# Block sums of the FFN in rooms shared with the mixers' tiles, first sums formed beside the output projections, input forms ordered behind the token factors

## The chip, the cores and the metric

One Trainium2 chip, one core of it. The metric is the device time of one execution in microseconds (us). The kernel before took 1460.63 us in the median of three runs (1458.15 to 1460.65). All times below that carry a position ("at 398.23") are microseconds from the start of the profiled execution's span.

## The reference, cut to what matters

Two layers on 528 tokens (16 learned meta tokens and 512 of the sequence) of width 1024, in float32. Layer 0 mixes tokens with forgetting attention (FoX, 16 heads of 64), layer 1 with a gated linear recurrence (HGRN2, 8 heads of 128). Behind each mixer stands a gated MLP with a causal convolution of width 3 (hidden width 2816):

```python
for layer in range(DEPTH):
    if layer % 2 == 0:
        h = h + fox_attention(h, ...)      # ends in o @ w_out
    else:
        h = h + hgrn2_mixer(h, ...)        # ends in o @ w_out
    h = h + conv_ffn(h, ...)
return h[:, N_META:]

def conv_ffn(h, ...):
    xn = rms_norm(h, norm_g)
    a = conv_b + causal_dwconv3(xn @ w_gate)
    return (silu(a) * (xn @ w_up)) @ w_down
```

## The kernel before

Activations stand transposed in SBUF: `h` is 128 partitions x 8 blocks x 528 tokens. Every projection is done in split precision: a weight block is loaded into a tile `raw` (SyncE's DMA queue), ScalarE (ACT) casts it to `hi`, VectorE (DVE) forms `lo = raw - hi` (`sub`, L127), and TensorE (PE) multiplies hi by the high part of the input, hi by the low part and lo by the high part (`proj_unit`, L209, L212, L213). There are two rooms for `raw` and three each for `hi` and `lo`, of 128x1024, which the FFN cuts in halves of 128x512.

The program is traced in the order fox, ffn 0, hgrn, ffn 1; the framework's scheduler then lays every instruction into its engine's queue, by program order, dependences and its own simulated timeline. An engine works through its queue strictly in that order, and so do the DMA queues that SyncE (SP) and GpSimd (POOL) issue. `self.after(ins, prev)` adds an order between two instructions that the scheduler must keep.

A mixer ends in an output projection over 8 row blocks m, each with 128x1024 weights `wo` or `ho` (fox: the last loop over m, which calls `out_proj` at L662; the first halves of four blocks are done earlier, at L615; hgrn: the loop behind the last `stage_o`). Each block's result is added to `h`, and `sumsq(m)` builds the squares for the next norm.

The FFN begins with `token_stats` (L301 matmuls give the mean squares; twelve small DVE instructions and a copy into `rst`, L311, give each token's factor 1/rms) and `spread_rs` (L322 matmuls spread the factors over partitions, L324 copies them into `rsb`). The columns of the hidden layer are then worked in pairs. The first pair is done by `plain`: for m = 0, 1 the gate products over 8 blocks in a PSUM bank "s" (`pss`, of which there are four; "p", `psp`, has two; "c" and "d" one each), then DVE multiplies each half by `rsb` into `A` (L1208), the convolution follows, then the up products (L1217). All later pairs go through `seven`: a 2x2 block product in seven products instead of eight (Strassen's scheme, as in Winograd's form), L1143 to L1145. It needs two things more:

- input forms: sums and differences of blocks of `h`, `input_forms(k)` for k = 0 to 3: two ACT scalings, one DVE subtraction (L1071), two DVE instructions (L1075), a cast to `xfhi` and a subtraction into `xflo`;
- weight sums: sums of blocks of the weights, formed by DMA alone in `make_sums`: SP loads one block into a tile `sum` (L1110, 256 KB), then POOL issues a DMA that adds a second block onto it (L1111), the second block from memory or from another sum. Twelve such tiles have a pool of their own, opened with the FFN. Each `next(making)` brings one or two sums; `plain` calls it five times, and `seven` three times for each of its jobs.

At the start of the FFN the rest of SP's queue is therefore made of blocks for `plain` (`raw<-gu`, L1096), a down block (`raw<-dn`) and the first sums.

Of the kernel before, what the change touches and what calls it, by code (L numbers as in the profile page):

```python
# [12 lines left out]
F32 = mybir.dt.float32  # L13
F32R = mybir.dt.float32r
# [3 lines left out]
ALU = mybir.AluOpType  # L18
# [3 lines left out]
P = 128  # L22
D = 1024
KT = D // P
T = 528
# [3 lines left out]
NEARLY = 4  # L29
NSUMS = 12  # L30
PAIRS = [1, 2, 2, 2, 2, 2]
HALF = KT * P // 2
FF = 2816
NF = FF // P
# [49 lines left out]
class Builder:  # L84
# [44 lines left out]
    def setup(self):  # L129
        nc = self.nc  # L130
        cp = self.cp = self.pool("const")
        self.h = cp.tile([P, KT, T], F32, name="h")
        self.vec = cp.tile([P, V_END], F32, name="vec")
        nc.sync.dma_start(self.vec, self.a["vec"])
        self.wraw = self.pool("wraw", 2)
        self.whi = self.pool("whi", 3)
        self.wlo = self.pool("wlo", 3)
        q, k = (self.weights(self.a["wqk"][0, i], KT, parts=2) for i in range(2))
        order = [(q, 0), 0, (k, 0), 1, 2, 3, (q, 1), (k, 1), 4, 5, 6, 7]
        for x in order:  # L140
            if isinstance(x, int):
                nc.sync.dma_start(self.h[:, x, :], self.a["h0"][:, x, :])
            else:
                x[0][3][x[1]]()
        self.first = q[:3], k[:3]
        cst = cp.tile([P, C_END], F32, name="cst")
        self.cst = cst
        nc.sync.dma_start(cst, self.a["cst"])
        self.ident = cst[:, C_ID : C_ID + P]
        self.identr = cp.tile([P, P], F32R, name="identr")  # L150
        nc.vector.tensor_copy(self.identr, self.ident)
        self.xhi = cp.tile([P, KT, T], F32R, name="xhi")
        self.xlo = cp.tile([P, KT, T], F32R, name="xlo")
        self.x = [(self.xhi[:, k, :], self.xlo[:, k, :]) for k in range(KT)]
        self.rsb = cp.tile([P, T], F32, name="rsb")
        self.onesd = cp.tile([P, 2], F32, name="onesd")
        nc.vector.memset(self.onesd, 1.0 / D)
        self.tiny = self.pool("tiny", 2)
        self.sqp = self.pool("sqp", 2)
        self.ps = self.pool("ps", 1, PSUM)  # L160
        self.nbank = 0
        self.ss = None

    def anybank(self):
# [14 lines left out]
    def weights(self, src, n, w=P, parts=1):  # L179
# [19 lines left out]
        return *u, [partial(load, slice(i * m, i * m + m)) for i in range(parts)]  # L199

    def proj_unit(self, ps, units, x, t0, tn, prev=None):

        mm = self.nc.tensor.matmul
        total = sum(u[2] for u in units)
        k = 0
        for hi, lo, n in units:
            for i in range(n):
                xh, xl = (y[:, t0 : t0 + tn] for y in x[k])
                ins = mm(ps, hi[:, i, :], xh, start=k == 0, stop=False)  # L209
                if k == 0 and prev is not None:  # L210
                    self.after(ins, prev)
                mm(ps, hi[:, i, :], xl, start=False, stop=False)  # L212
                mm(ps, lo[:, i, :], xh, start=False, stop=k == total - 1)  # L213
                k += 1
                if k % 2 == 0:
                    yield 0.66

    def lone(self, pool, gcol, t0):

        x = pool.tile([P, KT, 32], F32, name="lone")  # L220
        g = self.vec[:, gcol : gcol + KT].rearrange("p (k o) -> p k o", o=1)
# [74 lines left out]
    def token_stats(self, segs, last=False, bank=None):  # L296
# [13 lines left out]
        y = self.rsqrt(am, "n")  # L310
        nc.vector.tensor_copy(rs, y)  # L311
        return am, rs
# [14 lines left out]
    def fox(self, ctx):  # L327
# [8 lines left out]
        for kt in range(KT):  # L336
            self.sumsq(kt, 0, nc.gpsimd, s2)
        lone = self.lone(sp, V_FOXN, T - 32)
        identb = sp.tile([P, P], BF16, name="identb")
# [236 lines left out]
        for i in range(NSLOT):  # L576
            pk = sp.tile([P, 4, T], F32R, name=f"pk_{i}", tag=f"pk_{i}")
            d = {n: pk[:, j, :] for j, n in enumerate(("k1", "q1", "k2", "q2"))}
# [37 lines left out]

        late = [sp.tile([P, T], F32, name=f"late_{i}") for i in range(4)]
        ox, gated = [], []
# [3 lines left out]
        for p in range(-3, NPAIR):  # L622
# [26 lines left out]
            while gated and p >= max(gated[0], 5 + gated[0] // 4):  # L649
# [5 lines left out]
                self.sub(olo, o, ohi.bitcast(F32))  # L655
                ox.append((ohi, olo))
        for m in range(KT):
            res = None
            if m >= NEARLY:
# [115 lines left out]
    def hgrn(self, ctx):  # L775
# [6 lines left out]
        ohi = sp.tile([P, KT, T], F32R, name="ohi")  # L782
        ogs, ox = [None] * KT, [None] * KT
        lmask = sp.tile([P, len(LEVELS) - 3, 64], I32, name="lmask")
        nc.sync.dma_start(lmask, a["lmask"])
# [39 lines left out]
        self.normsplit(V_HGN)  # L825
        lone = self.lone(sp, V_HGN, 0)
        am, rs = self.token_stats(SEGH)
# [4 lines left out]
        def stage_a(m):  # L832

            if m % 2 == 0:
                vv = s2.tile([P, 5, 2 * P], F32, name="vv", tag="vv", bufs=3)
                vals[m] = vals[m + 1] = vv
# [7 lines left out]
            f = s2.tile([P, T], F32, name="f", tag="f", bufs=3)  # L844
            kp = s2.tile([P, T], F32, name="kp", tag="kp", bufs=3)
            qp = s2.tile([P, T], F32, name="qp", tag="qp", bufs=4)
# [168 lines left out]
        for m in range(-3, KT):  # L1015
# [7 lines left out]
                (stage_g(g) if g else None, 5.4 * len(g)),  # L1023
            )
        for m in range(KT):
            wt = self.weights(a["ho"][m], KT)
            for t0, tn in late:
# [8 lines left out]
    def ffn(self, ctx, layer, a0, o0):  # L1036
# [10 lines left out]
        s2 = self.pool(f"ffn2_{layer}", 2, ctx=ctx)  # L1047
        sums = self.pool(f"sums_{layer}", 1, ctx=ctx)

# [14 lines left out]
        def input_forms(k):  # L1064
# [3 lines left out]
            for x, kt in ((u[:, 0:8:7, :], k), (u[:, 1:3, :], 4 + k)):  # L1068
                h = self.h[:, kt, g0:].rearrange("p (f t) -> p f t", t=gw)
                nc.scalar.activation(x, h, AF.Copy, scale=self.vcol(gcol + kt))  # L1070
            nc.vector.tensor_tensor(  # L1071
                u[:, 3:6:2, :], u[:, 0:3:2, :], u[:, 7:8, :].to_broadcast([P, 2, gw]), ALU.subtract
            )
            for i, x, y in ((4, 3, 2), (6, 4, 1)):
                nc.vector.scalar_tensor_tensor(u[:, i, :], u[:, x, :], -1.0, u[:, y, :], ALU.mult, ALU.subtract)  # L1075
# [22 lines left out]

        def hidden_blocks(job):

            j, i = job
            return [a[f"gu{layer}"][2 * j + m, i, k] for m in range(2) for k in range(2)]

        def make_sums():

            def new(job, f, x, y):
                s = sums.tile([P, HALF], F32, name="sum", tag="sum", bufs=NSUMS)
                nc.sync.dma_start(s, x)  # L1110
                nc.gpsimd.dma_start(s, y, accum_op=ALU.add)  # L1111
                made[job, f] = s

            for n_, job in enumerate([*jobs, None]):
                if job is not None:
                    w11, w12, w21, w22 = hidden_blocks(job)
                    new(job, 1, w21, w22)
                    new(job, 3, w11, w21)
                    yield
                if n_:  # L1120
                    new(jobs[n_ - 1], 4, hidden_blocks(jobs[n_ - 1])[1], made[jobs[n_ - 1], 2])
                    yield
                if job is not None:
                    new(job, 2, w11, made[job, 1])
                    yield

        jobs, made = [], {}
        making = make_sums()

        def seven(j, i, put):  # L1130
# [5 lines left out]
            job = j, i  # L1136
            w11, w12, _, w22 = hidden_blocks(job)

# [8 lines left out]

            u, v = block(w11), parts(made[job, 1])
            yield product(A, u, 0, True)
            nc.scalar.copy(B, A)  # L1150
            yield product(D, v, 3, True)
            put(1, 1, D, False)
            u, v = parts(made[job, 2]), block(w12)
            next(making, None)
            yield product(B, u, 4, False)
# [3 lines left out]
            put(0, 0, A, True)  # L1159
            u, v = parts(made[job, 3]), parts(made[job, 4])  # L1160
            next(making, None)
            yield product(C, u, 5, False)
# [3 lines left out]
            u = block(w22)  # L1166
            next(making, None)
            yield product(C, u, 6, False)
# [30 lines left out]
        def plain(j, out):  # L1199

            A, t = new_pair("A"), new_pair("t")[:, :, :n]
            for m in range(2):
                wg = [block(a[f"gu{layer}"][2 * j + m, 0, k]) for k in range(2)]
                next(making)
                for t0, tn in ga:
                    ps = self.bank("s")[:, :tn]
                    yield from self.proj_unit(ps, wg, self.x, t0, tn)
# [3 lines left out]
                wu = [block(a[f"gu{layer}"][2 * j + m, 1, k]) for k in range(2)]  # L1211
                next(making)
                for t0, tn in up:
# [4 lines left out]
                input_forms(2 * m + 1)  # L1218
            next(making)
            split(t, out)  # L1220
# [60 lines left out]
        for r in PAIRS:  # L1281
            runs.append((j0, r, []))
            j0 += r
        for j in range(PAIRS[0], NF // 2):
            jobs += [(j, 0)] if j == PAIRS[0] else []
            jobs += [(j + 1, 0)] if j + 1 < NF // 2 else []
            jobs += [(j, 1)]
        side = None
# [115 lines left out]
```

## Time and profile before

| | |
|---|---|
| three runs, us | 1458.15, 1460.63, 1460.65 |
| the profiled execution, us | 1461.63 |
| its span, us | 1459.8 |
| its mean granted PE clock | 0.992 |
| start of ffn 0 (L301 matmuls) | at 391.63 |
| start of ffn 1 (L301 matmuls) | at 1114.30 |

The span is the time between the first and the last instruction of the profiled execution; 1.8 us lie around it. In the windows of the profile, an engine's busy time in a stretch is followed by the number of instructions that touch it, then come the granted PE clock, the busy share of the 16 DMA engines (it can pass 1 where transfers of two queues overlap on an engine) and the rate. In the chain of waits and the timeline, each row is a start, a duration and what ran; "SPq" and "POOL ... DMA_DIRECT2D" are issues of transfers, "x7" says that neighbours of one kind are put together.

### The profile page before, as it was taken

What the parts mean: (1) busy time and instruction counts of PE and PEld (TensorE: products, weight loads), DVE (VectorE), ACT (ScalarE), POOL (GpSimd) and SP (SyncE); (2) the same over time, 40 slices, a digit from 0 to 9 for tenths busy, and PEclk for the clock granted to TensorE, in tenths of its full rate; (3) what the DMA queues carried; (4) which work ended last, traced back from release to release, by engine and by line L of the source; (5) the groups of instructions that cost most, each with busy time, mean ns of one, the idle gap of its engine ahead of it and who ended that gap; (6) DMA issues with size and microseconds to landing.
All of it is one profiled execution on the core that took longest, in us unless ns stands there. A gap on an engine that the chain in (4) does not pass through costs nothing.

```text
span 1459.8 us, 29803 instructions
## 1 busy us (share of the span) xinstructions
PE 1419.5 (97%) x11368; PEld 1338.7 (92%) x11368; DVE 1010.4 (69%) x2263; ACT 723.9 (50%) x1524; POOL 175.3 (12%) x280
## 2 busy tenths in 40 slices
PE   7999999999979999999999999999999999999999
PEld 6888888888979999999999999999999999999997
DVE  7555545775858877767775667677648887777774
ACT  5455555574636555554643224333436665555551
POOL 7000000000122221221000000000020221221100
PEclk9999999999989999999999999999999999999999
DMA  4433344412689998886322202121284899988823
GB/s 160 120 106 90 95 108 125 128 60 62 194 195 238 231 232 194 218 208 164 92 69 87 77 13 88 59 73 45 64 226 129 200 260 225 218 218 219 200 80 101
DMA packets 104887, 206.90 MB, mean 142 GB/s; under 512 B 14104, under 2 KB 16920, under 8 KB 104744
## 3 DMA queue, kind: packets, MB, share of 16 engines
q1 hardware_dynamic: 81704, 163.05, 36.7%
q0 software_dynamic: 23040, 41.95, 17.2%
q8 instruction: 89, 1.46, 0.4%
q14 instruction: 54, 0.44, 0.1%
HBM read 168.53 MB, written 2.10 MB: 117 GB/s over the span
## 4 chain that ended last, share of the span: by engine, by line
PE 90%; DMA 4%; DVE 2%; ACT 2%; SPq 1%; issue 1%; ACTq 0%; DVEq 0%
PE pss L209 7%; PE pss L212 7%; PE pss L213 7%; PE psp L209 7%; PE psp L213 7%; PE psp L212 7%; PE psp L258 6%; PE psp L1143 5%; PE psp L1144 5%; PE psp L1145 5%; PE psd L1143 3%; PE psd L1144 3%; PE psd L1145 3%; PE psc L752 2%; PE pss L906 1%; PE psc L1143 1%
## 5 line engine op out<-in xcount | busy, mean ns | idle before, releaser
L127 DVE TENSOR_TENSOR lo<-raw,hi 128x512 fp32r<-128x512 f32 (+2 forms) x318 | 254.4, 804 | 95.7 <-ACT hi L1089 50.3
L1089 ACT CAST hi<-raw 128x512 fp32r<-128x512 f32 (+1 forms) x232 | 139.1, 604 | 169.6 <-PE pss L212 53.8
L209 PE MATMUL psp<-xhi,hi 128*128 128x264 f32 (+2 forms) x752 | 216.8, 290 | 6.1 <-ACT xhi L278 6.1
L212 PE MATMUL psp<-xlo,hi 128*128 128x264 f32 (+2 forms) x752 | 216.9, 289 | 3.3 <-DVE xlo L279 3.3
L213 PE MATMUL psp<-xhi,lo 128*128 128x264 f32 (+2 forms) x752 | 217.2, 289 | 0.0
L212 PE MATMUL pss<-room,hi 128*128 128x264 f32 (+2 forms) x532 | 169.7, 320 | 0.0
L209 PE MATMUL pss<-room,hi 128*128 128x264 f32 (+2 forms) x532 | 168.8, 320 | 0.0
L213 PE MATMUL pss<-room,lo 128*128 128x264 f32 (+2 forms) x532 | 168.7, 319 | 0.0
L1089 ACT CAST hi<-sum 128x512 fp32r<-128x512 f32 x160 | 99.0, 619 | 111.8 <-PE psd L1144 42.0
L195 ACT CAST hi<-raw 128x1024 fp32r<-128x1024 f32 (+1 forms) x82 | 82.4, 1007 | 141.4 <-PE psp L212 59.8
L209 PEld LDWEIGHTS psp<-xhi,hi 128*128 128x128 f32 x752 | 142.6, 190 | 9.4 <-ACT xhi L278 6.1
L212 PEld LDWEIGHTS psp<-xlo,hi 128*128 128x128 f32 x752 | 142.8, 190 | 5.3 <-DVE xlo L279 3.8
L213 PEld LDWEIGHTS psp<-xhi,lo 128*128 128x128 f32 x752 | 142.8, 190 | 1.5 <-issue 1.5
L1143 PE MATMUL psp<-xhi,hi 128*128 128x264 f32 (+1 forms) x480 | 136.6, 285 | 1.7 <-ACT hi L1089 1.7
L1145 PE MATMUL psp<-xhi,lo 128*128 128x264 f32 (+1 forms) x480 | 136.3, 284 | 1.0 <-DVE lo L127 1.0
L1144 PE MATMUL psp<-xlo,hi 128*128 128x264 f32 (+1 forms) x480 | 136.2, 284 | 0.0
L127 DVE TENSOR_TENSOR lo<-sum,hi 128x512 fp32r<-128x512 f32 x160 | 109.5, 687 | 24.1 <-ACT hi L1089 20.8
L1111 POOL DMA_DIRECT2D sum<-gu x80 | 70.1, 886 | 352.7 <-PE psp L212 96.6
L213 PEld LDWEIGHTS pss<-room,lo 128*128 128x128 f32 x532 | 99.6, 188 | 6.5
L212 PEld LDWEIGHTS pss<-room,hi 128*128 128x128 f32 x532 | 100.0, 188 | 5.1
L209 PEld LDWEIGHTS pss<-room,hi 128*128 128x128 f32 x532 | 99.9, 188 | 4.2
L1270 DVE TENSOR_TENSOR h<-h,pss 128x264 f32<-128x264 f32 (+2 forms) x145 | 73.4, 508 | 35.8 <-PE pss L213 35.3
(442 smaller groups left out, 3961.2 us busy)
## 6 DMA issues: line engine op xcount, KB each, us to landing
sum<-gu SPq DMA_DIRECT2D x160, 256.0 KB
raw<-gu SPq DMA_DIRECT2D x136, 256.0 KB
sum<-gu POOLq DMA_DIRECT2D x80, 256.0 KB, 5.5
sum<-sum POOLq DMA_DIRECT2D x80, 256.0 KB, 5.2
raw<-dn SPq DMA_DIRECT2D x80, 256.0 KB
pk<-stg SPq DMA_DIRECT2D x48, 264.0 KB
raw<-wqk SPq DMA_DIRECT2D x14, 512.0 KB
raw<-wv SPq DMA_DIRECT2D x8, 512.0 KB
```

Of the source, the lines that this page charges most:

```text
L127: self.nc.vector.tensor_tensor(out, x, y, ALU.subtract)
L195: nc.scalar.copy(hi, raw)
L209: ins = mm(ps, hi[:, i, :], xh, start=k == 0, stop=False)
L212: mm(ps, hi[:, i, :], xl, start=False, stop=False)
L213: mm(ps, lo[:, i, :], xh, start=False, stop=k == total - 1)
L258: mm(ps[:tn, :256], y[:, t0 : t0 + tn], w, start=n == 0, stop=n == 23)
L1089: nc.scalar.copy(hi, raw)
L1111: nc.gpsimd.dma_start(s, y, accum_op=ALU.add)
L1143: mm(ps, hi[:, k, :], xh, start=start and k == 0, stop=False, skip_group_check=not start)
L1144: mm(ps, hi[:, k, :], xl, start=False, stop=False, skip_group_check=not start)
L1145: mm(ps, lo[:, k, :], xh, start=False, stop=k == 3, skip_group_check=not start)
L1270: nc.vector.tensor_tensor(hv, hv, ps, ALU.add)
```

## The change

A pool `shared` is opened once for the whole kernel: two tiles "two" of 128x2112 and one tile "one" of 128x1840 floats. The fox mixer uses them for two of its six head slots (`pk_2`, `pk_3`, which heads 14 and 15 use last), three of its four `late` tiles and `lone`; the hgrn mixer for its value tiles `vv`, its keys `kp` and `lone`. The FFN's own pool of twelve sums is gone: `make_sums` cuts the same three tiles into 4 + 4 + 3 = 11 rooms of 128x512.

`make_sums` is now started before the output projection of the mixer, and the loop over m calls `next` from m = 2 on (six calls); `plain` calls it no more. In `plain`, the gate products of m = 1 go to bank "p" instead of "s". The first DVE instruction of `input_forms` is ordered behind the copy into `rst`.

```diff
+        self.shared = self.pool("shared", 1)
...
+    def share(self, dtype=F32):
+        n = 4 * T
+        two = [self.shared.tile([P, n], dtype, name="two", tag="two", bufs=2) for _ in range(2)]
+        return *two, self.shared.tile([P, 3 * T + 256], F32, name="one", tag="one")
...
+    def make_sums(self, layer):
...
+        rooms = cycle(s[:, x : x + HALF] for s in self.share() for x in range(0, s.shape[1] - HALF + 1, HALF))
+        made = self.made = {}
+        def new(job, f, x, y):
+            s = made[job, f] = next(rooms)
+            nc.sync.dma_start(s, x)
+            nc.gpsimd.dma_start(s, y, accum_op=ALU.add)
...
         y = self.rsqrt(am, "n")
-        nc.vector.tensor_copy(rs, y)
+        self.stats = nc.vector.tensor_copy(rs, y)
...
-            pk = sp.tile([P, 4, T], F32R, name=f"pk_{i}", tag=f"pk_{i}")
+            if i in (2, 3):
+                pk = shared[i - 2].rearrange("p (a t) -> p a t", t=T)
+            else:
+                pk = sp.tile([P, 4, T], F32R, name=f"pk_{i}", tag=f"pk_{i}")
...
+        self.making = self.make_sums(0)
         for m in range(KT):
+            if m > 1:
+                next(self.making)
             res = None
...
+        self.making = self.make_sums(1)
         for m in range(KT):
+            if m > 1:
+                next(self.making)
             wt = self.weights(a["ho"][m], KT)
...
-            nc.vector.tensor_tensor(
+            ins = nc.vector.tensor_tensor(
                 u[:, 3:6:2, :], u[:, 0:3:2, :], u[:, 7:8, :].to_broadcast([P, 2, gw]), ALU.subtract
             )
+            self.after(ins, self.stats)
...
-                next(making)
                 for t0, tn in ga:
-                    ps = self.bank("s")[:, :tn]
+                    ps = self.bank("sp"[m])[:, :tn]
...
-                next(making)
                 for t0, tn in up:
...
-            next(making)
             split(t, out)
```

`make_sums` itself is otherwise as it was; in `seven` only `making` became `self.making`.

**SP at the end of fox.** The queue before, from the last head's rows (`lrow`) on: `wo` are the output projection's weights, `res` the residual input, `gu` and `dn` blocks of the FFN.

```order
L194 DMA raw<-wo 128x512
L720 DMA pk_258<-lrow 1x4x128 x2
L721 DMA pk_258<-lrow 2x16
L194 DMA raw<-wo 128x512 x2
L194 DMA raw<-wo 128x1024 x4
L1096 DMA raw<-gu 128x512 x2
L661 DMA res<-h 128x528
L1096 DMA raw<-gu 128x512 x2
L661 DMA res<-h 128x528
L1096 DMA raw<-gu 128x512 x4
L1110 DMA sum<-gu 128x512 x7
L1096 DMA raw<-gu 128x512
```

And of the change, where `two` and `one` are the shared tiles (L226 is the load of a sum, L1152 that of a block):

```order
L200 DMA raw<-wo 128x512
L226 DMA one<-gu 128x512 x2
L769 DMA two<-lrow 1x4x128 x2
L770 DMA two<-lrow 2x16
L226 DMA one<-gu 128x512
L200 DMA raw<-wo 128x512 x2
L226 DMA two<-gu 128x512 x8
L200 DMA raw<-wo 128x1024 x4
L1152 DMA raw<-gu 128x512
L710 DMA res<-h 128x528
L1152 DMA raw<-gu 128x512 x3
L710 DMA res<-h 128x528
```

Two loads of sums moved ahead of the last head's rows, and eight stand in a block ahead of the four large `wo` loads; the seven and five that stood among the FFN's blocks are gone from there.

**SP at the end of hgrn.** Before (`hg` and `ho` are the gate's and the output projection's weights):

```order
L194 DMA raw<-hg 128x1024 x8
L194 DMA raw<-ho 128x1024 x5
L1110 DMA sum<-gu 128x512 x11
L194 DMA raw<-ho 128x1024
L1110 DMA sum<-gu 128x512
L194 DMA raw<-ho 128x1024 x2
L1096 DMA raw<-gu 128x512 x9
```

And of the change:

```order
L200 DMA raw<-hg 128x1024 x7
L226 DMA one<-gu 128x512 x3
L200 DMA raw<-hg 128x1024
L200 DMA raw<-ho 128x1024 x2
L226 DMA two<-gu 128x512 x4
L200 DMA raw<-ho 128x1024
L226 DMA two<-gu 128x512 x4
L200 DMA raw<-ho 128x1024 x5
L1152 DMA raw<-gu 128x512 x9
```

The block of eleven sums ahead of the sixth `ho` load is spread over the loads before it.

**DVE at the start of ffn 0.** Before, from the second Newton step of the token factors on (`run`, `rqn` are its steps, `am` holds the mean squares):

```order
L127 TENSOR_TENSOR lo<-raw,hi 128x512
L291 TENSOR_TENSOR run<-rqn 128x6
L127 TENSOR_TENSOR lo<-sum,hi 128x512
L127 TENSOR_TENSOR xflo<-room,xfhi 128x4x264
L292 SCALAR_TENSOR_TENSOR run<-run,am 128x6
...
L305 MEMSET am 128x1
L311 COPY rst<-rqn 128x6
L324 COPY rsb<-psc 128x256
L127 TENSOR_TENSOR lo<-raw,hi 128x512
L324 COPY rsb<-psd 128x272
L1208 TENSOR_TENSOR A<-pss,rsb 128x264 x2
```

And of the change (L1126 and L1131 are the input forms, L353 and L366 the copies into `rst` and `rsb`, L1232 the multiplication into `A`):

```order
L347 MEMSET am 128x1
L353 COPY rst<-rqn 128x6
L1126 TENSOR_TENSOR room<-room 128x2x264 x4
L1131 SCALAR_TENSOR_TENSOR room<-room 128x264 x2
L126 TENSOR_TENSOR lo<-raw,hi 128x512
L1131 SCALAR_TENSOR_TENSOR room<-room 128x264 x2
L366 COPY rsb<-psc 128x256
L1131 SCALAR_TENSOR_TENSOR room<-room 128x264 x2
L366 COPY rsb<-psd 128x272
L126 TENSOR_TENSOR lo<-two,hi 128x512
L1131 SCALAR_TENSOR_TENSOR room<-room 128x264 x2
L1232 TENSOR_TENSOR A<-pss,rsb 128x264 x2
```

The input forms, which stood ahead of and between the steps of the token factors, follow the copy into `rst` in one block, most of it ahead of the copies into `rsb`.

More of the change, by code (lines that the diff above doesn't have):

```diff
@@ L29 @@
 NEARLY = 4
-NSUMS = 12
 PAIRS = [1, 2, 2, 2, 2, 2]
@@ L199, in weights, with hidden_blocks @@
         return *u, [partial(load, slice(i * m, i * m + m)) for i in range(parts)]
+    def hidden_blocks(self, layer, job):
+        j, i = job
+        return [self.a[f"gu{layer}"][2 * j + m, i, k] for m in range(2) for k in range(2)]
+    def make_sums(self, layer):
+        nc = self.nc
+        jobs = []
+        for j in range(PAIRS[0], NF // 2):
+            jobs += [(j, 0)] if j == PAIRS[0] else []
+            jobs += [(j + 1, 0)] if j + 1 < NF // 2 else []
+            jobs += [(j, 1)]
+        rooms = cycle(s[:, x : x + HALF] for s in self.share() for x in range(0, s.shape[1] - HALF + 1, HALF))
[4 more added lines that the diff above has]
+            nc.gpsimd.dma_start(s, y, accum_op=ALU.add)
+        for n, job in enumerate([*jobs, None]):
+            if job is not None:
+                w11, w12, w21, w22 = self.hidden_blocks(layer, job)
+                new(job, 1, w21, w22)
+                new(job, 3, w11, w21)
+                yield
+            if n:
+                ahead = jobs[n - 1]
+                new(ahead, 4, self.hidden_blocks(layer, ahead)[1], made[ahead, 2])
+                yield
+            if job is not None:
+                new(job, 2, w11, made[job, 1])
+                yield
     def proj_unit(self, ps, units, x, t0, tn, prev=None):
@@ L216, in proj_unit, with lone @@
                     yield 0.66
-    def lone(self, pool, gcol, t0):
-        x = pool.tile([P, KT, 32], F32, name="lone")
+    def lone(self, x, gcol, t0):
+        x = x.rearrange("p (k t) -> p k t", k=KT)
         g = self.vec[:, gcol : gcol + KT].rearrange("p (k o) -> p k o", o=1)
@@ L337, in fox @@
             self.sumsq(kt, 0, nc.gpsimd, s2)
-        lone = self.lone(sp, V_FOXN, T - 32)
+        shared = self.share(F32R)
+        lone = self.lone(shared[2][:, 3 * T :], V_FOXN, T - 32)
         identb = sp.tile([P, P], BF16, name="identb")
@@ L615, in stage_p @@
                 yield from out_proj(m, 0, 4, hold=True)
-        late = [sp.tile([P, T], F32, name=f"late_{i}") for i in range(4)]
+        late = [shared[2][:, i * T : i * T + T] for i in range(3)] + [sp.tile([P, T], F32, name="late")]
         ox, gated = [], []
@@ L783, in hgrn @@
         ogs, ox = [None] * KT, [None] * KT
+        w = 5 * 2 * P
+        shared = self.share()
+        vvs = cycle(x[:, :w].rearrange("p (t c) -> p t c", c=2 * P) for x in shared)
+        kps = cycle(x[:, w : w + T] for x in shared)
         lmask = sp.tile([P, len(LEVELS) - 3, 64], I32, name="lmask")
@@ L825, in hgrn @@
         self.normsplit(V_HGN)
-        lone = self.lone(sp, V_HGN, 0)
+        lone = self.lone(shared[0][:, w + T : w + T + 256], V_HGN, 0)
         am, rs = self.token_stats(SEGH)
@@ L834, in stage_a @@
             if m % 2 == 0:
-                vv = s2.tile([P, 5, 2 * P], F32, name="vv", tag="vv", bufs=3)
+                vv = next(vvs)
                 vals[m] = vals[m + 1] = vv
@@ L844, in stage_a @@
             f = s2.tile([P, T], F32, name="f", tag="f", bufs=3)
-            kp = s2.tile([P, T], F32, name="kp", tag="kp", bufs=3)
+            kp = next(kps)
             qp = s2.tile([P, T], F32, name="qp", tag="qp", bufs=4)
@@ L1047, in ffn @@
         s2 = self.pool(f"ffn2_{layer}", 2, ctx=ctx)
-        sums = self.pool(f"sums_{layer}", 1, ctx=ctx)
         rooms = {}
@@ L1097, in block @@
             return parts(raw)
[L1099 to L1128, printed above, removed]
         def seven(j, i, put):
@@ L1136, in seven @@
             job = j, i
-            w11, w12, _, w22 = hidden_blocks(job)
+            w11, w12, _, w22 = self.hidden_blocks(layer, job)
             def product(ps, unit, f, start):
@@ L1146, in product @@
                 return 1.45
-            u, v = block(w11), parts(made[job, 1])
+            u, v = block(w11), parts(self.made[job, 1])
             yield product(A, u, 0, True)
@@ L1152, in seven @@
             put(1, 1, D, False)
-            u, v = parts(made[job, 2]), block(w12)
-            next(making, None)
+            u, v = parts(self.made[job, 2]), block(w12)
+            next(self.making, None)
             yield product(B, u, 4, False)
@@ L1159, in seven @@
             put(0, 0, A, True)
-            u, v = parts(made[job, 3]), parts(made[job, 4])
-            next(making, None)
+            u, v = parts(self.made[job, 3]), parts(self.made[job, 4])
+            next(self.making, None)
             yield product(C, u, 5, False)
@@ L1166, in seven @@
             u = block(w22)
-            next(making, None)
+            next(self.making, None)
             yield product(C, u, 6, False)
@@ L1283, in ffn @@
             j0 += r
[L1284 to L1287, printed above, removed]
         side = None
```

## The prediction

> **What bounds the kernel now.** I read the page first: PE is busy 97% of the span and makes up 90% of the chain that ended last. The change leaves all arithmetic of PE as it was, so only time in which PE stands still or runs at a lower clock can be won.
>
> ```profile
> PE 1419.5 (97%) x11368; PEld 1338.7 (92%) x11368; DVE 1010.4 (69%) x2263; ACT 723.9 (50%) x1524; POOL 175.3 (12%) x280
> DMA  4433344412689998886322202121284899988823
> PE 90%; DMA 4%; DVE 2%; ACT 2%; SPq 1%; issue 1%; ACTq 0%; DVEq 0%
> sum<-gu POOLq DMA_DIRECT2D x80, 256.0 KB, 5.5
> ```
>
> The waits of PE, grouped by line, say where it stood still (total, times, longest):
>
> ```profile
> PE psd L1278 <- DVE rsb L324: 8.4, 1, 8.4
> PE pss L737 <- DMA pk<-lrow: 3.4, 1, 3.4
> PE psc L322 <- DVE rst L311: 2.3, 2, 2.1
> PE psc L1143 <- ACT psc L1150: 2.2, 1, 2.2
> PE psp L209 <- ACT hi L195: 0.9, 1, 0.9
> ```
>
> The first lies at the start of ffn 0, the second at the end of fox, 2.1 of the third at the start of ffn 1, the last at the end of hgrn. Windows over these places give the size (us; then busy time and instructions of PE, PEld, DVE, ACT, POOL; granted clock; DMA share; GB/s):
>
> ```profile
> 385.00:450.00 65.00, 52.73 (x409) 51.47 (x409) 44.28 (x89) 33.12 (x59) 16.97 (x23) 0.92 0.85 208
> 405.00:410.00 5.00, 1.16 (x10) 0.91 (x8) 0.42 (x1) 0.00 (x0) 0.89 (x2) 0.86 1.11 269
> 410.00:415.00 5.00, 0.44 (x1) 0.29 (x1) 1.50 (x4) 1.19 (x3) 2.65 (x3) 0.50 1.11 256
> 415.00:420.00 5.00, 5.00 (x27) 4.97 (x27) 2.49 (x5) 2.09 (x3) 0.87 (x1) 0.61 1.08 243
> 1080.00:1090.00 10.00, 8.34 (x67) 7.93 (x67) 2.83 (x4) 2.68 (x4) 2.65 (x3) 1.00 1.09 288
> 1120.00:1130.00 10.00, 7.95 (x53) 7.70 (x52) 7.16 (x22) 4.15 (x8) 1.73 (x2) 0.83 0.67 144
> 358.02 0.29 PE L212 MATMUL pss<-pk,hi 128*128 128x264 f32 x1
> 359.98 0.28 PE L212 MATMUL psp<-pk,hi 128*128 128x264 f32 x1
> ```
>
> The last two rows stand 16 matmuls apart: 1.96 / 16 = 0.1225 us a matmul at full clock. Ffn 0: 65 us hold 65 / 0.1225 = 531 matmuls, but the window has 409, so 122 x 0.1225 = **14.9 us are lost**. The other way: 65 - 52.73 = 12.3 idle, and 5 us at 0.61 and 0.44 at 0.50 cost 2.2 more, 14.5 together. Ffn 1: 10 - 8.34 = 1.7 idle at the `ho` weights, 10 - 7.95 = 2.05 at the token factors, and a clock of 0.83 over 10 us costs 1.7: **5.4 us**.
>
> Why ffn 0 stands still is shown by the chain there, and by the queues of SP and POOL (put together in the timeline):
>
> ```profile
> 398.23 14.50 DMA raw<-gu
> 412.81 0.63 ACT hi L1089
> 414.15 0.36 DVE rsb L324
> 387.17 3.44 SPq L1110 DMA_DIRECT2D sum<-gu  x7
> 391.61 3.26 SPq L1110 DMA_DIRECT2D sum<-gu  x5
> 396.04 5.87 SPq L1096 DMA_DIRECT2D raw<-gu  x3
> 392.84 0.17 DVE am L306
> 404.31 0.17 DVE L311 COPY rst<-rqn 128x6 f32<-128x6 f32 x1
> ```
>
> Twelve loads of sums went in front of the blocks `raw` at 396.04 and 398.23; with POOL's additions beside them the DMA share was 1.1 and a block took 14.5 us. DVE, in order, stood at that block's `lo` with the second `rsb` copy behind it, and PE waited for `rsb`. Besides, `rst` took from 392.84 to 404.31, because input forms stood between its steps.
>
> **The change, part by part.** All sums are against the profiled execution's own 1461.63 us (1.0 above the median of the runs; span 1459.8 and 1.8 around it).
>
> *Sums away from the start of ffn 0.* SP issues twelve loads and POOL their additions some 35 us sooner, beside the output projection. The late block is then loaded into a free queue, and the stall at `rsb` with its slow clock goes. What is late next is DVE: it was busy 44.28 us of the window, and 65 - 14.9 = 50.1 us would remain, 88% of it. Its new order puts most of the input forms as a block ahead of the `rsb` copies:
>
> ```profile
> L1071 DVE TENSOR_TENSOR room<-room 128x528 f32<-128x528 f32 x4 | 2.8, 703 | 0.4 <-ACT room L1070 0.4
> L1075 DVE SCALAR_TENSOR_TENSOR room<-room 128x264 f32<-128x264 f32 x8 | 3.3, 426 | 0.0
> L127 DVE TENSOR_TENSOR lo<-raw,hi 128x512 fp32r<-128x512 f32 x11 | 7.5, 686 | 10.2 <-ACT hi L1089 10.1
> ```
>
> 4 x 0.70 + 4 x 0.43 + 0.69 = 5.2 us. Without forms between its steps, `rst` needs its thirteen small instructions at 0.17 and two `lo` at 0.69, 3.6 us: 392.8 + 3.6 = 396.4, ahead of PE, which reaches L322's place after 53 matmuls at 391.6 + 6.5 = 398.1. The first `rsb` copy then ends at about 402 and the evacuations L1208 begin near 404; PE has 48 matmuls of m = 1 in the other bank until 398.1 + 5.9 = 404.0. That cover just holds; each us by which `rst` slips beyond it is a us of PE. With 2.2 (L1143 behind an ACT copy) perhaps left, I leave **2.5 us lost (0.5 to 8)**: -12.4.
>
> *The last head's rows.*
>
> ```profile
> 333.94 1.59 DMA pk<-lrow
> 332.84 0.41 SPq L720
> ```
>
> Two sum loads now issue just ahead of these rows: 0.41 of queue, and half a MB in front of rows that took 1.59. From +0.3 to +1.5; I take **+0.6**, nearer the issue row. PE waits there already, so nothing hides it.
>
> *The large `wo` loads behind eight sums.*
>
> ```profile
> 352.15 8.73 SPq L194 DMA_DIRECT2D raw<-wo  x2
> 358.59 1.59 ACT L195 CAST hi<-raw 128x512 fp32r<-128x512 f32 x2 [4.07 <-PE pss L212]
> q1 hardware_dynamic: 442, 0.82, 70.8%
> q0 software_dynamic: 1073, 1.94, 65.5%
> q1 hardware_dynamic: 1346, 2.36, 44.0%
> ```
>
> The first two: the load of m = 4 issued at 352.15, and its cast was the second of the two that ended at 360.2, so the data were no limit before. The `q` rows are SP's queue from 387 to 391 with little beside it (0.82 MB in 70.8% of 4 us: 0.29 MB/us), then both queues from 396 to 412 (SP 2.36 / 16 = 0.148 MB/us, additions 1.94 / 16 = 0.121). Now eight sums of 0.26 MB go first; they wait for the last reads of the heads' slots, near 349. 2.6 MB until m = 4 is in: at 0.29 alone, with 1.5 us until the first data, 349 + 1.5 + 9 = 359.5, no wait. At 0.148 throughout: 368, and PE, which needs it at 360.7 behind a cast of 1.05, would wait 8.4, and more with the clock: +10. In between: POOL's addition lands 5.5 us after its issue, of which 256 KB at 0.29 are 0.9, so additions start to share near 356; by then 1.6 MB are in, the other 1.0 takes 6.8: 362.8, PE at 363.9. That is 3.2 late; less 0.5 of slack, plus a chance of the half clock that followed such a wait: **+3.6 (0 to +10)**. The rest of the fox end has cover: a block of m is 48 matmuls, 5.9 us, and its 0.52 MB at 0.148 are 3.5.
>
> A page's rule on the price: the Trainium skill, "DMA: Bandwidth & Descriptors", section "Latency and other measured facts", gives a first byte about 1 us after a GpSimd issue. By it the additions would share from 353 on, m = 4 would land at 365.5, and this term would be about +6.5; the landing row's 5.5 us speaks against it.
>
> *Sums at the end of hgrn.* There they issue ahead of `ho` loads with tens of us to spare, and the stall of 1.7 goes; `rst` no longer stands behind input forms, and the 2.05 with their 1.7 of clock go. Both places keep DVE's block of forms; I leave 1 us (0 to 3): **-4.4**.
>
> On the clock: the row 1120 to 1130 shows a clock of 0.83 around a wait of 2.1 us. The Trainium skill, "TensorE: Matmul & The Clock Gate", "What's actually happening", has the lower clock after at least one idle window of about 3.4 us. By the page alone the 2.1 us would have cost no clock, and this term would be -2.7; the trace's row disagrees, and I go by the row.
>
> The shared rooms cost nothing elsewhere: each tile's readers end well before its next writer, except at the two places above. Eleven rooms in place of twelve matter in `seven` alone, where SP's order is unchanged.
>
> Sum: -12.4 + 0.6 + 3.6 - 4.4 = -12.6; 1461.63 - 12.6 = **1449.0 us**.
>
> **The rivals.**
>
> *The fox end costs nothing.* The sums are in before the additions share (359.5 above), and both starts close: 1461.63 - 14.4 + 0.3 - 5.4 = 1442, down to 1440. For it: the DMA digits of the page are 2 to 6 in the slices of the fox end. Against: 2.1 MB in one block.
>
> *The fox end gives half back.* 368 for m = 4: 1461.63 - 12.4 + 0.6 + 10 - 4.4 = 1455.4, up to 1457.5. For it: at 1.1 share SP's queue kept 0.148 for 16 us. Against: additions chain on one another and start late.
>
> *Slower: the jam moves, and ffn 0 keeps its stall.* From 349 to 388 SP has 2.9 MB of sums, 2.1 of `wo`, 0.5 of `res` and 2.4 of blocks to bring, 7.9 in all. Additions of 2.9 MB at 0.121 last 24 us, SP gets 3.6 MB in them, and the remaining 4.3 at 0.29 take 15: 39 us, to 388, just when ffn 0 needs its blocks. If the rates are lower than these, the blocks land past 400, the `lo` between the forms holds the `rsb` copies as before, and the loss of 14.9 stays on top of +10: 1461.63 + 0.6 + 10 - 4.4 = 1468. It decides from a landing of about 400 on. Against it: from 352 to 386 the page's DMA digits leave half of the engines free.
>
> *The change doesn't do what it says.* The stall of 14.9 was not the sums' doing but the FFN's own blocks, or DVE's 88% comes out as bound: the gain at ffn 1 is given back at fox: 1459 to 1463.
>
> **How the numbers follow.** Forecast (1444 to 1454) 0.55; nothing lost at fox (1440 to 1444) 0.15; half given back (1454 to 1457.5) 0.14; no net effect 0.07; slower 0.09. About 0.2%, 2.9 us, is what a measurement of this kernel can tell from no change. Faster by more: 0.55 + 0.15 + 0.14 = 0.84; within: 0.07; slower: 0.09. The range 1440 to 1457 takes in the first three but for their edge.
>
> **What would show it.** In the changed profile the wait for `rsb` is gone or under 2 us and `rst` is done by 397; the DMA share from 396 to 412 is well under 1.1; the wait of PE for a cast of `wo` m = 4 near 361 is 2 to 4 us; the 0.9 of L195 at the `ho` weights and the 2.1 for `rst` at ffn 1 are gone. Wrong I would be if the blocks `raw` of ffn 0 land past 400, if PE waits for `rsb` or a `seven`'s inputs behind DVE for more than 5 us, or if any of m = 5 to 7 at fox waits too.

## The result, and the profile after

| | before | changed |
|---|---|---|
| median of 14 runs each, us | 1461.97 | 1453.31 |
| lowest to highest, us | 1458.15 to 1466.43 | 1449.56 to 1459.86 |
| span of the profiled execution, us | 1459.8 | 1450.8 |

The ratio is 0.9944 with a 95% interval of 0.9931 to 0.9958: some 8 us faster. The forecast was 12.6 us, with a range of 1440 to 1457 us in which 1453.31 lies. The page of the changed kernel shows PE's work as it was and its share of the span a little larger, and traffic moved forward: the ninth to twelfth DMA digits (end of fox, start of ffn 0) go from 1, 2, 6, 8 to 2, 4, 7, 5, the 29th and 30th (end of hgrn) from 2, 8 to 6, 4:

```profile
PE 1419.9 (98%) x11368; PEld 1337.9 (92%) x11368; DVE 1009.5 (70%) x2263; ACT 723.0 (50%) x1524; POOL 176.0 (12%) x280
DMA  4433344424759898886322202222643799989833
```

The waits of PE that bear on the argument (the longest, of some 6 us, is in both kernels and not among them), and the windows at the start of ffn 0 and behind the start of ffn 1 (line numbers are the changed kernel's: L786 is the last head's L737, L251 and L1168 to L1170 are the products of L209 and L1143 to L1145):

```profile
PE pss L786 <- DMA two<-lrow: 4.2, 1, 4.2
PE psp L1168 <- ACT hi L1145: 2.7, 5, 0.6
PE psp L251 <- ACT hi L201: 1.3, 1, 1.3
PE psd L1168 <- ACT psd L1181: 1.3, 1, 1.3
PE psp L1170 <- DVE lo L126: 1.1, 2, 0.9
PE psp L1168 <- ACT A L1254: 0.7, 1, 0.7
385.00:450.00 65.00, 63.06 (x516) 62.43 (x515) 55.34 (x108) 42.52 (x77) 8.63 (x14) 1.00 0.59 151
1136.00:1146.00 10.00, 8.60 (x47) 6.59 (x45) 6.87 (x12) 4.26 (x9) 1.76 (x2) 1.00 0.82 197
```

From 385 to 450 PE now has 516 matmuls where it had 409, at full clock, and the 8.4 us for `rsb` are gone; so are the 2.1 for `rst` at ffn 1. New are a longer wait at the last head's rows, one for `wo` of m = 4, and a handful behind the starts of ffn 0 and ffn 1.

To place the difference, I took PE's matmuls in their order and, for each, how much later the next began than the median distance of its shape; the sum over a stretch is the time PE lost in it (us, one execution each). Some kernels of the experiments below have, up to a place or from a place on, the same order in every queue as the changed kernel. What these lost there stands in the last column:

| stretch, by matmuls | before | changed | others with the changed order |
|---|---|---|---|
| last head's rows (2420 to 2560) | 5.8 | 7.7 | 6.5 to 9.2 (seven) |
| `wo` of m = 4 (2560 to 2695) | 0 | 1.5 | 1.1 to 4.0 (seven) |
| start of ffn 0 (2695 to 3950) | 15.4 | 3.7 | 2.6 (one) |
| `ho` weights (8700 to 9050) | 2.5 | 0.2 | 0.2 (two) |
| start of ffn 1 (9050 to 9600) | 3.9 | 4.1 | 3.0 and 3.9 |

The differences between the two profiles are +1.9, +1.5, -11.7, -2.3 and +0.2: -10.4 together. The span is 9.0 shorter; 1.0 of the rest was lost ahead of matmul 2400, where both programs have the same order (other executions lay there from 1.0 early to 1.6 late of the one before). The last column says how far such a table can be read: at one place, executions of one order lie up to 3 us apart. The drops at ffn 0 and at the `ho` weights are far beyond that or recur every time; a difference of 1 or 2 us elsewhere, between two single executions, is not yet an effect.

### The profile page after: what moved, and what is told of

Its sections match the earlier page's. It is cut to its first block, busy times and chain, and to the rows that moved or that the text cites. A ratio compares the mean times of both kernels' runs of the same rounds, so it can differ in the third digit from the quotient of the medians.

```text
span 1450.8 us, 29750 instructions
## 1 busy us (share of the span) xinstructions
PE 1419.9 (98%) x11368; PEld 1337.9 (92%) x11368; DVE 1009.5 (70%) x2263; ACT 723.0 (50%) x1524; POOL 176.0 (12%) x280
## 4 chain that ended last, share of the span: by engine, by line
PE 91%; DMA 3%; DVE 2%; ACT 2%; issue 1%; SPq 1%; DVEq 0%; ACTq 0%
PE pss L251 7%; PE pss L254 7%; PE pss L255 7%; PE psp L251 7%; PE psp L254 7%; PE psp L255 7%; PE psp L300 6%; PE psp L1168 5%; PE psp L1170 5%; PE psp L1169 5%; PE psd L1168 3%; PE psd L1169 3%; PE psd L1170 3%; PE psc L801 2%; PE pss L959 1%; PE psc L1168 1%
## 5 line engine op out<-in xcount | busy, mean ns | idle before, releaser
L251 PE MATMUL psp<-xhi,hi 128*128 128x264 f32 (+2 forms) x784 | 226.1, 290 | 6.3 <-ACT xhi L320 6.3
L254 PE MATMUL psp<-xlo,hi 128*128 128x264 f32 (+2 forms) x784 | 226.5, 289 | 2.7 <-DVE xlo L321 2.7
L255 PE MATMUL psp<-xhi,lo 128*128 128x264 f32 (+2 forms) x784 | 226.8, 289 | 0.0
L1145 ACT CAST hi<-raw 128x512 fp32r<-128x512 f32 (+1 forms) x232 | 139.0, 604 | 170.3 <-PE pss L254 59.9
L251 PE MATMUL pss<-room,hi 128*128 128x264 f32 (+2 forms) x532 | 168.1, 320 | 0.0
L251 PEld LDWEIGHTS psp<-xhi,hi 128*128 128x128 f32 x784 | 148.9, 190 | 9.7 <-ACT xhi L320 6.3
L254 PEld LDWEIGHTS psp<-xlo,hi 128*128 128x128 f32 x784 | 149.2, 190 | 4.9 <-DVE xlo L321 3.4
L255 PEld LDWEIGHTS psp<-xhi,lo 128*128 128x128 f32 x784 | 149.3, 190 | 1.6 <-issue 1.5
L1168 PE MATMUL psp<-xhi,hi 128*128 128x264 f32 (+1 forms) x480 | 136.5, 284 | 3.4 <-ACT hi L1145 2.7
L1170 PE MATMUL psp<-xhi,lo 128*128 128x264 f32 (+1 forms) x480 | 136.2, 284 | 1.1 <-DVE lo L126 1.1
L1145 ACT CAST hi<-two 128x512 fp32r<-128x512 f32 x118 | 73.0, 619 | 84.9 <-PE psd L1169 32.4
L251 PEld LDWEIGHTS pss<-room,hi 128*128 128x128 f32 x532 | 99.5, 188 | 4.2
L1168 PEld LDWEIGHTS psp<-xhi,hi 128*128 128x128 f32 x480 | 90.6, 189 | 6.5 <-ACT hi L1145 4.0
L1168 PE MATMUL psd<-xfhi,hi 128*128 128x264 f32 (+1 forms) x320 | 90.9, 284 | 2.0 <-ACT psd L1181 1.3
```

Of the source, the lines that this page charges most:

```text
L1145: nc.scalar.copy(hi, raw)
L1168: mm(ps, hi[:, k, :], xh, start=start and k == 0, stop=False, skip_group_check=not start)
L1170: mm(ps, lo[:, k, :], xh, start=False, stop=k == 3, skip_group_check=not start)
```

## The experiments

Ratios are to the kernel before, timed on the same chip; in brackets is the 95% interval. Most intervals are some 0.003 wide, so the time does not tell neighbours of the changed kernel's 0.9944 apart. A profile is one execution, so of the profiles too I rest only on what is large or recurs.

**Which part brings the gain?** First the change without the order edge:

```diff
-            self.after(ins, self.stats)
```

> Sums formed early as in the change, but the input forms may again stand between the steps of the token factors. If the early sums are the gain at ffn 0 (the transfers no longer jam there), the wait for rsb stays short and the kernel keeps more than half of the gain: ratio to before 0.995 to 0.998, with PE waiting 2 to 4 us for rst at each of the two FFN starts. If the order edge is the gain, the ratio is 1.000 within 0.002 and a stall of about 8 us is back at the start of ffn 0.

1451.26 us, 0.9929 [0.9917, 0.9942]: better than both expectations. At ffn 0 PE waits 1.5 us for `rst`, not 2 to 4, and loses 2.5 in all; at ffn 1 it waits 0.9 for `rsb` and not for `rst`. Then the edge alone, on the kernel before (the three lines that keep the instruction, and the `after`):

```diff
+        self.stats = nc.vector.tensor_copy(rs, y)
...
+            self.after(ins, self.stats)
```

> The kernel before with the order edge alone; the sums still start with the FFN and their twelve rooms stay. If the jam of transfers is the cause of the stall at ffn 0, a block still takes over 10 us to land past 400, DVE stands at its lo, and the gain is only the 2 us for rst at ffn 1 and its clock: ratio 0.996 to 1.000. If the late token factors are the cause, ffn 0 gains 8 us or more: ratio 0.992 to 0.995.

1463.45 us, 1.001 [1.0001, 1.0019], just outside the first expectation. The stall at ffn 0 is in another place now: 14.5 us are lost. Nor did ffn 1 gain: the wait for `rst` is gone there, but PE waits 2.7 us for `rsb` and `A` instead. Waits of PE at ffn 0, windows, and the chain there (the kernel before, so L1209 is the multiplication into `A`):

```profile
PE pss L209 <- DVE A L1209: 6.6, 2, 5.8
PE psc L1144 <- ACT psc L1151: 3.1, 1, 3.1
410.00:415.00 5.00, 5.00 (x44) 5.00 (x43) 2.44 (x4) 0.00 (x0) 3.02 (x4) 1.00 1.10 283
415.00:420.00 5.00, 1.48 (x13) 1.27 (x11) 0.00 (x0) 0.50 (x1) 1.39 (x2) 0.85 1.14 208
395.95 9.73 DMA sum<-gu
412.52 6.90 DMA sum<-sum
419.50 0.63 ACT hi L1090
```

The token factors are early, and PE gets further; but a sum that took 9.73 us to load and an addition that took 6.90 hold ACT's and DVE's queues, DVE does nothing from 415 to 420, and PE stands. Without the move 15.4 us are lost at ffn 0, or 14.5 with the edge; with the move 2.5, or 3.7 with the edge. **The move of the sums is the gain, the edge adds none that shows.** The shared rooms belong to the move; no run separates the two.

**The second bank.** `self.bank("sp"[m])` back to `self.bank("s")`:

> The change with the gate products of m = 1 in bank s again. The prediction gave this edit no term: ratio to before the same as that of the change, 0.9944 within 0.0015. If the second bank is what carries PE over the forms ahead of rsb, PE waits again for rsb or A at ffn 0 by 2 us or more and the ratio is above 0.996.

1455.53 us, 0.9955 [0.9942, 0.9968], not to be told from the change by its time. The start of ffn 0 loses 5.4 where the change loses 3.7, with no wait for `rsb`. At ffn 1 PE waits 1.7 for `rsb` and 1.0 for `A`, which the change does not, and the start loses 5.8 for 4.1. So the bank is at most a small part of the gain.

**The edge for half of the forms.**

```diff
+            if k > 1:
+                self.after(ins, self.stats)
```

> The order edge for the forms of k = 2 and 3 alone; those of k = 0 and 1 may run while DVE waits for the mean squares (in the change DVE is idle for some 4.5 us there, and then busy without a break for 40 us). If the rest of the loss at both FFN starts is DVE's backlog, 2 to 4 us come back over both: ratio 0.9915 to 0.9935. If the rest is late blocks or PSUM evacuations on ACT, nothing changes: 0.9944 within 0.001.

1455.86 us, 0.9960 [0.9947, 0.9973]: outside both expectations. Its profile lost 6.1 us at 500 to 510, far behind the forms, where the change lost 0.1: a block took 6.64 us to land, its cast stood in ACT's queue ahead of a copy from PSUM to PSUM, and PE waited for the copy.

```profile
497.04 6.64 DMA raw<-gu
504.23 0.61 ACT hi L1146
504.84 0.29 ACT psc L1176
```

**The end of fox.** All loads of sums ordered behind the last head's rows on SP's queue:

```diff
+            if layer == 0:
+                self.after(ins, self.hold)   # ins: the load of a sum; hold: the last lrow DMA
```

> The change with all loads of sums ordered behind the last head's rows on SP's queue (two stood ahead of them). If those two loads are what lengthens the wait at the last head's rows (4.2 us, 3.4 before, and a longer stretch at half clock, 2.0 us in all by the matmuls' places), 1 to 2 us come back: PE's wait there 3.3 to 3.6 us, ratio to before 0.9925 to 0.9940. If the rows land late for another reason, the wait stays at 4.2 and the ratio at 0.9944.

1452.21 us, 0.9929 [0.9912, 0.9946], as the first expectation has it. PE's wait there is that of before, and its loss too (5.6):

```profile
PE pss L788 <- DMA two<-lrow: 3.4, 1, 3.4
PE psp L253 <- ACT hi L201: 2.1, 1, 2.1
```

The same with `hold` as the load of `wo` for m = 4, and `next` called twice each for m = 5, 6, 7:

> The change with all eleven loads of sums behind the load of wo for m = 4. If the eight sums ahead of it make PE wait there, that wait (1.3 us) goes and m = 4 is as early as before. The eleven then stand ahead of m = 5 to 7, whose rooms come free some 8 us later: by the rates of the prediction they cover it, and the ratio is 0.991 to 0.994. If the additions share the engines then, PE waits 1 to 4 us for m = 5 or 6 instead, and the ratio is 0.994 to 0.997.

1451.96 us, 0.9931 [0.9916, 0.9946]: the ratio of the first expectation with the wait of the second. The wait at m = 4 is gone, and 2.6 us are lost at m = 5 instead:

```profile
PE pss L791 <- DMA two<-lrow: 3.4, 1, 3.4
PE pss L253 <- ACT hi L201: 1.6, 1, 1.6
PE pss L257 <- DVE lo L126: 0.5, 1, 0.5
```

So the sums and their additions cost PE something at whichever `wo` load stands behind them: 1.1 to 4.0 us at m = 4 in the eight profiles with the change's order there, and at m = 5 here 2.6, in two later runs 4.0 and, with one sum fewer, 1.0.

**Is DVE's backlog what remains at the two starts?** In the changed kernel DVE is busy 37.84 of the 40 us from 400 on and 25.41 of the 26 from 1110 on. The four subtractions into `xflo` moved to POOL:

```diff
-            self.sub(xflo[:, :, k, :], u[:, 3:7, :], xfhi[:, :, k, :].bitcast(F32))
+            nc.gpsimd.tensor_tensor(xflo[:, :, k, :], u[:, 3:7, :], xfhi[:, :, k, :].bitcast(F32), ALU.subtract)
```

> The change with the four subtractions into xflo of each FFN start on POOL (1.25 us each on DVE; POOL took 1.60 us for a 128x528 sum, so some 3.2 each there). If DVE's backlog is what gives back the gain behind both FFN starts (DVE is busy without a break from 400 to 440 and from 1110 to 1136), 5 us of DVE at each start turn into 2 to 4 us of PE over both: ratio 0.9915 to 0.9935. If the rest is set by ACT's queue and late blocks, nothing: 0.9944 within 0.001.

1464.08 us, 1.002 [1.0007, 1.0032]: a loss, and no test of the backlog, because DVE stood still beside POOL. The timeline of POOL and DVE, and PE's longest wait (4.2 at ffn 0, 6.5 at ffn 1):

```profile
413.81 5.18 POOL L1133 TENSOR_TENSOR xflo<-room,xfhi 128x1056 fp32r<-128x1056 f32 x2
413.75 5.80 DVE L126 TENSOR_TENSOR lo<-two,hi 128x512 fp32r<-128x512 f32 x1
PE pss L251 <- ACT room L1212: 10.7, 2, 6.5
```

A DVE subtraction of 128x512, 0.69 elsewhere, lasted until POOL's two subtractions were done and some 0.6 us longer. Without the edge as well:

> As the run before, but without the order edge of the input forms. Two loads off DVE at once: if DVE is the bound and the edge only moves its work into the busy stretch, this is the fastest so far: ratio 0.990 to 0.9925, with no wait for rst over 2 us. If the edge is needed to keep the token factors early, rst is late by 2 to 3 us at ffn 0 and the ratio is 0.993 to 0.995.

1458.99 us, 0.9982 [0.9971, 0.9993], outside both expectations. PE waits 8.5 us for `rst` at the two starts; from 400 to 412 DVE is busy 11.80 us with 14 instructions, beside 10.13 of POOL:

```profile
PE psc L364 <- DVE rst L353: 8.5, 2, 5.6
400.00:412.00 12.00, 6.39 (x53) 6.21 (x52) 11.80 (x14) 3.44 (x5) 10.13 (x4) 0.92 0.16 45
```

So I lightened DVE without loading POOL, by leaving out three of the four subtractions:

```diff
+            if k == 0:
                 self.sub(xflo[:, :, k, :], u[:, 3:7, :], xfhi[:, :, k, :].bitcast(F32))
...
-                return xfhi[:, f - 3, k, :], xflo[:, f - 3, k, :]
+                return xfhi[:, f - 3, k, :], xflo[:, f - 3, 0, :]
```

> The change with one subtraction into xflo at each FFN start in place of four; the products with the sums of the input use the low parts of the first for all four (three low parts are left out). That takes 3 x 1.25 us off DVE at each start and nothing onto another engine. If DVE's backlog gives back the gain there, the waits of PE at 429 to 436 and near 1145 shrink: 2 to 4 us over both, ratio to before 0.9915 to 0.9935. If late blocks hold ACT's queue whatever DVE does, PE still waits there and the ratio stays at 0.9944 within 0.001.

1453.47 us, 0.9937 [0.9919, 0.9954], as the second expectation has it. With 3.75 us less of DVE at each start, ffn 0 loses 3.5, and 2.9 of it between matmuls 3185 and 3238, where the change and three others (the two runs with sums moved back at fox, and the one with a fifth room below) lose 2.8. At ffn 1 it loses 6.5. There the long wait of the change is twice as long, and its chain names a block:

```profile
PE psd L1169 <- ACT psd L1182: 2.7, 1, 2.7
...
1138.26 0.69 DVE lo L126
1138.97 5.02 DMA raw<-gu
1144.54 0.61 ACT hi L1146
1145.47 0.37 ACT psd L1182
```

At ffn 0, then, DVE's backlog as such is not what is left. At ffn 1 a piece of it is: between matmuls 9150 and 9200 the change and the same three others lose 1.6 each, behind the block of forms, and this kernel 0.5. The larger piece is another: a block that could be loaded only when a `lo` had freed its room, and whose cast stands ahead of the copy, holds PE.

**Copy first.** In the first two pairs behind `plain`, the second block of a `seven` is loaded as early as before, but cast behind the copy:

```diff
-            u, v = parts(self.made[job, 2]), block(w12)
+            u = parts(self.made[job, 2])
+            raw = ...                              # load of w12
...
+            c = nc.scalar.copy(C, B)
+            v = parts(raw, c)                      # cast ordered behind c
```

> The change with ACT's cast of the second block of a seven, for the first two pairs behind plain, ordered behind the copy from PSUM to PSUM which that cast stood in front of. If the wait near 1145 (1.3 us, and what follows) is a late block holding that copy in ACT's queue, it goes, and 1 to 2 us come back at ffn 1; the products behind may wait up to 1 us for the later cast: ratio 0.992 to 0.9945. If the copy is late for its own inputs, the wait stays and the ratio is 0.9944 to 0.996.

1465.93 us, 1.0013 [1.0001, 1.0026]: worse than either expectation. The wait for the copy in `psd` is still there, and PE waits for casts behind it. From ffn 0 on the scheduler laid all queues in another order than the change's, so this is not a clean test of the one cast. Its waits at ffn 1:

```profile
PE pss L251 <- ACT room L1221: 3.4, 1, 3.4
PE psd L1170 <- ACT psd L1188: 1.9, 2, 1.7
PE pss L251 <- ACT hi L1145: 1.4, 1, 1.4
```

**Two edits together.** Sums behind `wo` of m = 4, and no edge:

> The two edits that came out at or below the change, together: all loads of sums behind wo of m = 4, and no order edge of the input forms. If their effects add (fox end -3 us by the places of the matmuls, the edge -2 by the medians), the ratio is 0.990 to 0.992. If rst is late again by 1.5 us or more and the starts only trade stalls, 0.992 to 0.994.

1452.28 us, 0.9921 [0.9906, 0.9937], at the edge between the two expectations; `rst` is late by the 1.5 us of the second. The profile can't say whether the effects add: its execution took 1456.95 us, the longest of the six. In it 7.8 us are lost from matmul 2695 to 3450, 4.0 of them at m = 5 and 3.9 around a wait of 1.5 for `rst`, so the starts trade stalls here.

**A fifth room for blocks.** As the sums behind `wo`, and

```diff
+        *rooms, self.fifth = [...]               # ten rooms for sums
+            more = [self.fifth] if nm == "raw" else []
```

> The change with all loads of sums behind wo of m = 4 (as in that run before), and one of the eleven shared rooms given to the blocks: five rooms of 128x512 for raw in place of four, ten for sums. If the wait near 1142 comes from a block whose load could not be issued until a DVE lo freed its room, the load goes out a room earlier, the wait for the copy in psd (0.7 to 2.7 us in the runs so far) is under 0.5 us, and the ratio is 0.990 to 0.993. If the load is slow because additions share the engines, the wait stays and the ratio is that of the run without the fifth room, 0.9931 within 0.0015; ten rooms for sums may then cost up to 2 us more.

1448.64 us, 0.9921 [0.9907, 0.9935], the lowest median, but by its ratio no better than the run before. The wait for `psd` is gone. All waits of PE from 1110 to 1200:

```profile
PE psp L1175 <- ACT A L1261: 0.7, 1, 0.7
PE psp L1175 <- ACT hi L1152: 0.5, 1, 0.5
PE psd L1177 <- DVE lo L126: 0.5, 1, 0.5
PE psp L1177 <- DVE lo L126: 0.3, 1, 0.3
```

But that the room did it is not shown: in the run with the sums behind the rows, whose queues have the change's order from ffn 0 on, that wait was 0.2, below the 0.7 to 2.7 of the expectation, with four rooms. And the loss from matmul 9050 to 9600 is 4.3, no less than the change's 4.1: 1.6 behind the block of forms again, and 2.3 near 1139, where the chain names a block of the down projection that took 2.89 us to land. Of the 4.1 us by which this profile's span is shorter than the change's, 2.0 lie ahead of matmul 2400, where the order is the same. Its interval overlaps the change's.

## Why the prediction was right, and where it was not

*Sums away from ffn 0: -12.4 forecast, -11.7 measured.* Mechanism and size hold. The DMA share from 396 to 412 is 0.24 for 1.10. `rst` needs 3.3 us from `am`, for 3.6 forecast, and PE does not wait for it. That it is done at 400.6 and not by 397 is because the whole start lies 4.4 later:

```profile
397.28 0.17 DVE L348 TENSOR_SCALAR am<-psd 128x5 f32<-128x5 f32 x1 [3.00 <-PE psd L343]
400.45 0.17 DVE L353 COPY rst<-rqn 128x6 f32<-128x6 f32 x1
q1 hardware_dynamic: 576, 1.05, 20.6%
q0 software_dynamic: 27, 0.06, 3.1%
```

The `q` rows are the queues from 396 to 412: 1.11 MB where there were 4.3. The 2.5 us that I left there came, between the matmuls where the kernel before waited for the copy of L1143 (3185 to 3238); but PE waits for casts and a `lo` there now, not for that copy, so that the size fits is in part luck. One reason I gave weight to was idle, too: the early `rst`. Run without the edge, it was late again, and the start lost no more: 2.7 around the wait for `rst`, and nothing at 3185 to 3238. The forms only changed places.

*The last head's rows: +0.6 forecast, +1.9 between the two profiles.* The wait itself is as forecast. The rows left SP some 0.3 later behind the two loads and took 2.23 us for 1.59, and PE waits 4.2 for 3.4. In all eight profiles with two sums ahead of the rows this wait is 3.7 to 4.3, and in all six with none it is 3.4: +0.3 to +0.9.

```profile
333.17 0.81 SPq L226 DMA_DIRECT2D one<-gu  x2
335.31 2.23 DMA two<-lrow
330.00:345.00 15.00, 10.75 (x70) 9.66 (x66) 5.42 (x13) 3.88 (x9) 1.02 (x1) 0.77 0.39 102
330.00:345.00 15.00, 11.64 (x84) 10.84 (x83) 6.82 (x17) 5.07 (x13) 0.00 (x0) 0.89 0.12 36
```

The rest of the +1.9 is clock: 0.77 from 330 to 345, 0.89 in the kernel before (the last row). It does not follow from the longer wait. The edge alone on the kernel before has 0.77 with a wait of 3.4, and the edge for half of the forms 0.89 with 4.0. Over all these profiles the stretch lost 7.8 in the mean with two sums ahead and 6.6 with none.

*`wo` of m = 4 behind eight sums: +3.6 forecast, +1.5 measured, 1.1 to 4.0 over the eight profiles.* From the first of the eight issues to the landing of m = 4 it took 12.2 us (351.68 to 363.89), for 13.8 in the forecast. The runs with the sums behind it showed the wait to be their doing.

```profile
351.68 3.65 SPq L226 DMA_DIRECT2D two<-gu  x8
354.92 1.76 POOL L227 DMA_DIRECT2D two<-gu  x2 [16.57 <-DMA two<-gu]
355.42 8.47 DMA raw<-wo
363.99 1.05 ACT hi L201
```

The additions began to share the engines later than I had them: their first packet is at 359.02, 4.1 us after the issue at 354.92, for 356 in the forecast. In the 6 us before it SP's queue moved 1.79 MB, 0.30 MB/us for 0.29. No run shows the 1.5 us that I took until the first data; the first packet came 0.95 after the issue. By the price that the Trainium skill gives for a first byte after a GpSimd issue ("DMA: Bandwidth & Descriptors", "Latency and other measured facts") the landing would have come 16.5 us after the first issue (349 to 365.5 in the forecast); the 12.2 here and the 4.1 speak against it. PE's wait was 1.3 here and 1.0 to 2.3 over the eight, for the 2 to 4 that I had named; it drew no half clock here, and did so in others (last section).

*The end of hgrn and ffn 1: -4.4 forecast, -2.1 between the two profiles. This is the term that failed.* The `ho` part came (-2.3, and 0.2 left in each of the runs with the sums moved). The 2.1 us for `rst` and the half clock behind it went too, as forecast. The block of forms cost what "both places keep DVE's block of forms; I leave 1 us (0 to 3)" allows: 1.6. What the term left out is a late block whose cast holds up a copy from PSUM; with it the stretch loses 4.1 now, 3.9 before. The chain of the changed kernel there:

```profile
1140.58 0.70 DVE lo L126
1141.30 3.91 DMA raw<-gu
1145.75 0.38 ACT psd L1181
1146.17 0.39 PE psd L1168
```

The largest loss at one wait, 1.4 us, is a block late behind its room, in front of a copy in ACT's queue. In two other profiles with the same order in ffn 1 that wait is 0.2 and 0.7 and the stretch loses 3.0 and 3.9, so its size differs from one execution to the next. Nor is that block alone: with a fifth room its wait was gone and 4.3 were lost in pieces. How the 1.5 to 2.5 us behind the block of forms could be won is not settled by these runs; lighter DVE, an earlier copy and an earlier block have each been tried, one at a time.

In the profile 9.0 us came where 12.6 were forecast. Of the 3.6 missing, 2.3 are ffn 1, 1.3 the rows and 0.7 ffn 0, against 2.1 better at `wo`; the other 1.4 lie where the two programs have the same order. The forecast's sum is thus helped by an error at `wo` that offsets the one at ffn 1. Of the rivals, "gives half back" had the right places at fox, at 3.4 us in all instead of 10.6; the jam did not move (the blocks were in time); and the price of 14.9 at ffn 0 was the sums' doing.

## What to carry to other kernels

Transfers that a later stage needs belong beside an earlier stage with free queues, but each place where they enter SP's queue has its price in what stands behind them: look for small latency-bound rows there first, since a wait there is hidden by nothing and can drop PE's clock as well. When a stall of several us goes, expect the next queue to take a part: here a late block, its cast and a copy behind it in one in-order queue. One profiled execution shows such pieces by place. But executions of one order differ by up to 3 us at a place, so before a piece of that size is explained, look whether it recurs in other runs with the same order; neither such a piece nor the time, with intervals of 0.3%, could rank the variants here.

## What was not expected

DVE stood still beside POOL: while two subtractions of 128x1056 ran on POOL (5.18 us), a DVE subtraction of 128x512 took 5.80 us, 0.69 elsewhere. Work given to POOL beside a busy DVE took the ratio from 0.9944 to 1.002. And an edit that only keeps some late casts behind an urgent copy took it to 1.0013; in its profile other products wait for casts, in queues that the scheduler had laid anew.

The length of a wait does not say what it costs in clock. At `wo` of m = 4, a wait of 1.8 us in the run with bank s was followed by a clock of 0.66 (365 to 370), one of 2.1 us in the run with the sums behind the rows by none lower than 1.00.
